# Feed-forward inputs with one 512-column matmul and one of 256 in place of three of 256, in a two-block network on one core

## The chip, the core and the metric

The kernel runs on one core of a Trainium2 chip. TensorE multiplies matrices, VectorE (DVE in the profile) and ScalarE (ACT) work on elements, GpSimd (POOL) and SyncE (SP) mostly issue transfers. The metric is the device time of one execution in microseconds, lower being better; "time" is the median of three executions.

## The reference

Two blocks of depth 2 run one after the other on an activation of 256 tokens x 1024 features in float32. Each block layer has a mixer (the first block: a bidirectional mLSTM and a dilated attention; the second: a bidirectional state-space scan and a windowed attention with grouped keys) and a gated feed-forward part. What the change touches most is the feed-forward part; in both blocks it takes two products of the same activation and multiplies them:

```python
def swiglu(u, w1, w3, w2):                       # first block
    return (jax.nn.silu(u @ w1) * (u @ w3)) @ w2

        h = rms_norm(x, norm2_w[i])              # second block
        g, u = jnp.split(h @ w_up[i], [D_FF_2], axis=-1)
        g = depthwise_conv_centered(g, ffn_conv_w[i], ffn_conv_b[i])
        x = x + (jax.nn.silu(g) * u) @ w_down[i]
```

The width of the feed-forward part is 2816, or 22 tiles of 128. The windowed attention of the second block is the other place:

```python
        s = jnp.einsum("bqgrd,bkgd->bgrqk", qb, kb,
                       preferred_element_type=jnp.float32) * scale + bias
```

with 16 query heads of 64 dimensions on 4 key heads.

## The kernel before

**Precision.** A matmul operand is split in two: `hi`, the value rounded to the type that TensorE takes in one pass (written by ScalarE), and `lo`, the rest (written by VectorE, line 473). A product is three matmuls: hi x hi, hi x lo, lo x hi (`mm3`, lines 519 to 522). The names in the profile say which is which: for weights `hi` and `lo`, for the activation of a stage `uh` and `ul`.

**Weights.** All weights come as a list of chunks of 1 MB (`raw`, three buffers), in the order of a plan (`make_plan`). `chunk` makes sure that the two chunks after the one being used have been loaded and split. Chunks of kind "ada" are reduced on VectorE (line 412) instead of being multiplied on TensorE; in the first layer there are 12 of them among the 22 + 11 chunks of the feed-forward part.

**Order.** A scheduler orders each engine's instructions when the program is built, by priority (the order in the text, moved by the tables `PRIO1` and `PRIO2`) and by when its model expects operands to be there. At run time each engine works through its list in that order. In the mixers, small steps (scores, transposes, state-space products) are put between the large linear products by hand (`tick`, `pump`).

**Feed-forward inputs.** `ffn_in` (line 1341) walks over 20 chunks (f = 2 to 21; the first two tiles come from another place). A chunk holds the two weight tiles of one f, each of 8 k-tiles of 128 x 128. `lin_st` makes both products into one PSUM bank of 512 columns (`lbank`, four of them), the first into columns 0 to 255, the second into 256 to 511, 48 matmuls of 256 columns in all, with the weight as the stationary operand and 256 tokens as the moving one. `tail` (line 1366 for the first block, 1843 for the second) then makes the gate out of the bank and writes the parts of the result (`ffh`, `ffl`). The tail's tiles have 1 KB per partition and come from buffers shared by size: five of 1 KB in the first block, four in the second (`SHARED1`, `SHARED2`).

**Feed-forward outputs.** `unit` (lines 612 to 614, bank `ffo`) makes them with the activation as the stationary operand and 512 weight columns as the moving one.

**Attention scores of the second block** (`score`, lines 1644 to 1661): `q2t` holds, for even and for odd heads, the rounded query in the head's own 64 rows and the rest of it in the other 64. `kst` holds the rounded keys in both halves, so that one matmul over 128 rows (line 1652) gives two of the three products. The third (line 1653) multiplies the own 64 rows with the rest of the keys (`kl`), which is there once.

**Groups.** The transposes of probabilities (`mpt`, `qtr`), the products of the state-space part (`sy`, line 1573), of the windowed attention (`qo`, line 1705) and of the dilated one (`ao`) are groups of small matmuls whose operands are made one after another, for head 0 before head 1, for tokens 0 to 127 before 128 to 255. "sy", "qo", "qrt" and "ao" write 64 output columns of the array per matmul; the profile shows this as a stationary operand of 128*64, where others have 128*128 and line 1653 has 64*128. A float32 operand that is not split gives two instructions per matmul.

Of the kernel before, what the change touches and what calls it, by code (L numbers as in the profile page):

```python
# [10 lines left out]
F32 = mybir.dt.float32  # L11
F32R = mybir.dt.float32r
AF = mybir.ActivationFunctionType
ALU = mybir.AluOpType
# [34 lines left out]
SHARED2 = {512: 3, 1024: 4, 2048: 11, 3072: 5, 4096: 2}  # L49

C_ID, C_TU, C_TL, C_MK = 0, 128, 256, 384
N_CST = 384 + 512
# [252 lines left out]
def two_blocks_kernel(ctx: ExitStack, tc: tile.TileContext, a: dict, out: bass.AP, stop=None):  # L305
# [7 lines left out]
    pools = ExitStack()  # L313
    cur = {"tp": pools.enter_context(tc.tile_pool(name="tmp1", bufs=2)), "shared": SHARED1}
# [33 lines left out]
    mk = cst[:, C_MK:C_MK + 512]  # L348
# [13 lines left out]
    for l in range(DEPTH):  # L362
        pv1.append(cp.tile([P, a["pv1"].shape[2]], F32, name=f"pv1_{l}"))
        pv2.append(cp.tile([P, a["pv2"].shape[2]], F32, name=f"pv2_{l}"))
        rw2.append(cp.tile([P, 80], F32, name=f"rw2_{l}"))
    S.dma_start(pv1[0], a["pv1"][0])

    def late_params():
        S.dma_start(cst[:, P:], a["cst"][:, P:])
# [153 lines left out]

    def half_views(half, n):
# [251 lines left out]
    def new_u():  # L776
        uh = big("uh", F32R)
        ul = big("ul", F32R)
        return uh, ul
# [169 lines left out]
    def mixer1(l, u, ob0=None, small=None, begun=None):  # L949
# [78 lines left out]
        def head(h, qT, kT, v):  # L1028
# [42 lines left out]
            def trans():  # L1071
                tr = bank("mpt")
                for tt in range(2):
# [129 lines left out]
        def slots(j, qk):  # L1203
# [50 lines left out]
            def pv_():  # L1254
                o = bank("ao")
                for k, g, t0, n, vk in ((0, 0, 0, T, 0), (1, 0, 0, T, 1), (0, 1, 0, P, 0), (0, 1, P, P, 1),
                                        (1, 2, 0, P, 0), (1, 2, P, P, 1)):
                    for i in range(2):
                        c0 = (2 * j + i) * 64
                        PE.matmul(o[64 * i:64 * i + 64, t0:t0 + n], va[g][:, vk, c0:c0 + 64],  # L1260
                                  s["t", i, g > 0][:, k, t0:t0 + n], start=(k, g) == (0, 0), stop=(g, t0) == (2, P))
# [79 lines left out]
    def ffn_in(kind, l, u, outs, tail, mid=None):  # L1341
        prios["now"] = {}
        for f, ps in enumerate(outs):
            tail(f, ps)
        for f in range(2, NF):
            tail(f, lin_st(chunk(kind, l, f), u)[0])
# [16 lines left out]
    def ffn1(l, u, outs):  # L1363
        act = ff_tiles()

        def tail(f, ps):
            th = tmp([T], "fth")
            S.activation(th, ps[:, :T], AF.Tanh, scale=0.5)
            V.scalar_tensor_tensor(th, th, 1.0, ps[:, :T], ALU.add, ALU.mult)
            gt = tmp([T], "fgt")  # L1370
            V.tensor_tensor(gt, th, ps[:, T:], ALU.mult)
# [68 lines left out]
    def mixer2(l, u, zouts, small):  # L1440
# [95 lines left out]
        def ssd_quarter(i, xt):  # L1536
# [26 lines left out]
            def prod(pr):  # L1563
                def run():
# [5 lines left out]
                    for d, c, m0, l0, n in ((0, 0, 0, 0, T), (1, 1, P, 0, T), (0, 1, T, P, P), (1, 0, 0, 0, P)):  # L1570
                        for k in range(2):
# [48 lines left out]
        kl = tmp([2, T], "kl", F32R)  # L1620
# [3 lines left out]
        def attn(c):  # L1624
# [17 lines left out]
            def score(i):  # L1642
                def run():
                    hd = 4 * c + i
                    p = i % 2
                    own = slice(64 * p, 64 * p + 64)
# [125 lines left out]
        def keys():  # L1772
            ps = st("k2")
            for p in range(2):
# [4 lines left out]
                V.tensor_tensor(kl[own], src, kst[p][own].bitcast(F32), ALU.subtract)  # L1779
# [59 lines left out]
    def ffn2(l, u, outs):  # L1839
# [4 lines left out]
        def tail(f, ps):  # L1844
            acc = tmp([T], "fgt")
            g0 = ps[:, :T]
# [8 lines left out]
            V.tensor_tensor(gt, th, ps[:, T:], ALU.mult)  # L1855
# [62 lines left out]
```

## Time and profile before

| | |
|---|---|
| time, median of three | 1934.13 us (1933.36 to 1936.22) |
| profiled execution | 1935.3 us |
| its span, first to last instruction | 1933.5 us |
| granted TensorE clock, mean | 0.997 of full speed |
| TensorE, matmuls | 1890.2 us busy, 13022 instructions |
| VectorE | 1465.9 us busy |
| ScalarE | 1085.0 us busy |
| moved by DMA | 388 MB, 201 GB/s on average |

A row of the profile that names a line of the kernel gives the engine, the operation, the tiles that it writes and reads, and their shapes. Matmuls overlap in the array, so the durations of neighbouring rows add up to more than the time they take; the distance from start to start is what a matmul costs. The stretches of the feed-forward inputs in the span are 394 to 509, 939 to 1057, 1348 to 1461 and 1750 to 1865 us; the main parts of the second block's mixers are 1186 to 1310 and 1586 to 1712 us.

### The profile page before, as it was taken

What the parts mean: (1) busy time and instruction counts of PE and PEld (TensorE: products, weight loads), DVE (VectorE), ACT (ScalarE), POOL (GpSimd) and SP (SyncE); (2) the same over time, 40 slices, a digit from 0 to 9 for tenths busy, and PEclk for the clock granted to TensorE, in tenths of its full rate; (3) what the DMA queues carried; (4) which work ended last, traced back from release to release, by engine and by line L of the source; (5) the groups of instructions that cost most, each with busy time, mean ns of one, the idle gap of its engine ahead of it and who ended that gap; (6) DMA issues with size and microseconds to landing.
All of it is one profiled execution on the core that took longest, in us unless ns stands there. A gap on an engine that the chain in (4) does not pass through costs nothing.

```text
span 1933.5 us, 32684 instructions
## 1 busy us (share of the span) xinstructions
PE 1890.2 (98%) x13022; PEld 1710.4 (88%) x13022; DVE 1465.9 (76%) x2555; ACT 1085.0 (56%) x1881; POOL 87.5 (5%) x108
## 2 busy tenths in 40 slices
PE   6999999999999999999999999999999999999998
PEld 5889999899978899999899888778998898779996
DVE  8888877787767787868766578877876688768763
ACT  3556654454436566544544457876554577756552
POOL 0000000200010000000200001000000000000000
PEclk9999999999999999999999999999999999999999
DMA  8654777487745446767377636444555454345552
GB/s 313 253 185 161 265 248 275 154 292 287 272 153 196 175 169 222 249 255 261 137 272 281 230 111 181 132 128 174 196 192 183 171 184 152 107 169 188 192 179 86
DMA packets 64202, 388.09 MB, mean 201 GB/s; under 512 B 7611, under 2 KB 12395, under 8 KB 21554
## 3 DMA queue, kind: packets, MB, share of 16 engines
q1 hardware_dynamic: 58064, 364.93, 52.3%
q0 software_dynamic: 4832, 20.13, 3.5%
q8 instruction: 102, 1.67, 0.3%
q10 hardware_dynamic: 1154, 0.95, 0.2%
q14 instruction: 50, 0.41, 0.1%
HBM read 384.82 MB, written 5.36 MB: 202 GB/s over the span
## 4 chain that ended last, share of the span: by engine, by line
PE 88%; DVE 5%; ACT 3%; DMA 1%; issue 1%; POOL 0%; POOLq 0%; DVEq 0%; ACTq 0%
PE lst L520 17%; PE lst L521 17%; PE lst L522 17%; PE ffo L613 4%; PE ffo L612 4%; PE ffo L614 4%; PE wo L612 2%; PE wo L613 2%; PE wo L614 2%; PE sy L1573 2%; PE qs L1653 1%; PE qo L1705 1%; PE avl L553 1%; PE avl L554 1%; PE avl L555 1%
## 5 line engine op out<-in xcount | busy, mean ns | idle before, releaser
L473 ACT ACTIVATE hi<-raw 128x1024 fp32r<-128x1024 f32 x546 | 571.7, 1057 | 499.0 <-PE lst L521 302.0
L473 DVE TENSOR_TENSOR lo<-raw,hi 128x1024 fp32r<-128x1024 f32 x546 | 662.5, 1221 | 229.5 <-ACT hi L473 228.7
L520 PE MATMUL lst<-uh,hi 128*128 128x256 f32 x2592 | 743.9, 287 | 0.0
L522 PE MATMUL lst<-uh,lo 128*128 128x256 f32 x2592 | 737.8, 285 | 0.2
L521 PE MATMUL lst<-ul,hi 128*128 128x256 f32 x2592 | 737.9, 285 | 0.0
L520 PEld LDWEIGHTS lst<-uh,hi 128*128 128x128 f32 x2592 | 496.6, 192 | 5.1 <-issue 3.9
L522 PEld LDWEIGHTS lst<-uh,lo 128*128 128x128 f32 x2592 | 496.7, 192 | 4.5 <-issue 3.5
L521 PEld LDWEIGHTS lst<-ul,hi 128*128 128x128 f32 x2592 | 496.8, 192 | 3.3 <-issue 2.1
L412 DVE CUSTOM_DVE_ANT_0 raw<-raw,crow,pv 128x1024 f32<-128x1024 f32 x96 | 120.9, 1280 | 27.6 <-DMA raw<-in_ws_dram 27.5
L612 PE MATMUL ffo<-hi,ffh 128*128 128x512 f32 x352 | 137.3, 390 | 0.0
L613 PE MATMUL ffo<-lo,ffh 128*128 128x512 f32 x352 | 137.0, 389 | 0.0
L614 PE MATMUL ffo<-hi,ffl 128*128 128x512 f32 x352 | 137.0, 389 | 0.0
L942 DVE SCALAR_TENSOR_TENSOR cacc<-cin,pv,cacc 128x254 f32<-128x254 f32 (+2 forms) x272 | 111.6, 478 | 0.3 <-ACT cacc L935 0.2
L614 PEld LDWEIGHTS ffo<-hi,ffl 128*128 128x128 f32 x352 | 66.1, 188 | 13.7
L612 PEld LDWEIGHTS ffo<-hi,ffh 128*128 128x128 f32 x352 | 66.1, 188 | 13.5
L613 PEld LDWEIGHTS ffo<-lo,ffh 128*128 128x128 f32 x352 | 66.1, 188 | 13.5
L774 DVE TENSOR_TENSOR ul<-uf,uh 128x256 fp32r<-128x256 f32 (+1 forms) x35 | 26.4, 755 | 26.7 <-ACT uh L769 26.7
L1555 ACT ACTIVATE sM<-arow,ac 128x128 f32<-128x128 f32 x128 | 44.9, 389 | 0.0
L1402 ACT ACTIVATE rsq<-xres 128x512 f32<-128x512 f32 x20 | 12.5, 627 | 53.3 <-DVE xres L1865 21.6
L553 PE MATMUL mvh<-hi,uh 128*128 128x512 f32 x80 | 33.4, 418 | 8.1 <-ACT uh L865 8.1
L555 PE MATMUL ltt<-hib,ul 128*128 128x512 f32 x72 | 29.7, 413 | 7.7 <-DVE ul L774 5.5
L766 ACT ACTIVATE uf<-tr,ub,us 128x128 f32<-128x128 f32 x36 | 14.3, 451 | 39.9 <-PE tr L752 39.9
(381 smaller groups left out, 3004.4 us busy)
## 6 DMA issues: line engine op xcount, KB each, us to landing
raw<-in_ws_dram SPq DMA_DIRECT2D x329, 1024.0 KB, 4.9
abias<-in_bt_dram SPq DMA_DIRECT2D x32, 256.0 KB, 4.7
arow<-scra POOLq DMA_DIRECT2D x32, 256.0 KB, 5.4
wtab<-skew SPq DMA_DIRECT2D x16, 384.0 KB, 3.6
gb<-in_rows_dram POOLq DMA_DIRECT2D x8, 512.0 KB, 5.8
skew<-scrt POOLq DMA_DIRECT2D x4, 1024.0 KB, 11.9
raw<-in_ws_dram SPq DMA_DIRECT2D x6, 512.0 KB, 8.9
grow<-scrg POOLq DMA_DIRECT2D x2, 1024.0 KB, 6.3
```

Of the source, the lines that this page charges most:

```text
L412: V.tensor_tensor_reduce(src, src, crow, 1.0, pv1[l][:, 136 + sec * 8 + ct:137 + sec * 8 + ct], ALU.mult, ALU.add, ada[l, sec][:, ct:ct + 1])
L473: fn()
L520: PE.matmul(outp, sh, mh, start=first, stop=False)
L521: PE.matmul(outp, sh, ml, start=False, stop=False)
L522: PE.matmul(outp, sl, mh, start=False, stop=last)
L553: PE.matmul(outs[tt], sl[0], hi[:, i, :], start=kt == first, stop=False)
L555: PE.matmul(outs[tt], sl[1], hi[:, i, :], start=False, stop=kt == last)
L612: PE.matmul(o, sh, hi[:, i, :], start=kt == first, stop=False)
L613: PE.matmul(o, sh, lo[:, i, :], start=False, stop=False)
L614: PE.matmul(o, sl, hi[:, i, :], start=False, stop=kt == last)
L942: V.scalar_tensor_tensor(acc[:, c, lo:hi], src[:, lo + s:hi + s], cw[:, k0 + j:k0 + j + 1], acc[:, c, lo:hi], ALU.mult, ALU.add)
L1555: S.activation(m[:, d, 2 * tt * P:(2 * tt + 1) * P], rt[:, d, hh, tt * P:(tt + 1) * P], AF.Relu, scale=-1.0, bias=ac[:, tt, col])
```

## The change

Three things change.

1. The activation of a stage is kept with the two parts of a k-tile side by side (`Acts`): 256 columns of the rounded part, then 256 of the rest. In `ffn_in` a new routine (`lin_wide`) multiplies the rounded weight with both at once, one matmul of 512 columns into a whole bank, and the rest of the weight with the rounded part, one of 256 columns into the first half of the bank. Each of the chunk's two products has its own bank, one from each of the two PSUM pools (four banks each). `wide_sum` then adds the two halves of a bank into a new 1 KB tile: ScalarE copies the second half, VectorE adds the first.
2. The rest of the keys (`klt`) is kept in both halves of the rows, once for even and once for odd heads, and line 1653's matmul takes all 128 rows. The tile that this needs comes from a twelfth 2 KB buffer; its space is won by putting the mask `mk` and the first block's parameters `pv1` into a pool that is given back before the second block. The mask has a transfer of its own.
3. Five groups of small matmuls run in the other order, so that their first instruction reads what is made last.

```diff
-SHARED2 = {512: 3, 1024: 4, 2048: 11, 3072: 5, 4096: 2}
+SHARED2 = {512: 3, 1024: 4, 2048: 12, 3072: 5, 4096: 2}
...
+    class Acts:
+        def __init__(self, name, n=8):
+            self.tiles = [big(name, F32R, (P, 4, 2, T)) for _ in range(n // 4)]
...
+        def both(self, kt):
+            return self.tiles[kt // 4][:, kt % 4]
...
+    def lin_wide(w, u):
+        banks = []
+        for half, pool in zip(w, (lbank, bank)):
+            hi, lo = half_views(half, P)
+            banks.append(pool("lsw"))
+            for kt in range(8):
+                with prio("lin"):
+                    PE.matmul(banks[-1], hi[:, kt, :], u.both(kt), start=kt == 0, stop=False)
+                    PE.matmul(banks[-1][:, :T], lo[:, kt, :], u[0][:, kt, :], start=False, stop=kt == 7)
+        return banks
+
+    def wide_sum(banks):
+        res = []
+        for b in banks:
+            res.append(tmp([T], "lss"))
+            S.activation(res[-1], b[:, T:], AF.Copy)
+            V.tensor_tensor(res[-1], b[:, :T], res[-1], ALU.add)
+        return res
...
-        uh = big("uh", F32R)
-        ul = big("ul", F32R)
-        return uh, ul
+        return Acts("u")
...
         for f in range(2, NF):
-            tail(f, lin_st(chunk(kind, l, f), u)[0])
+            tail(f, wide_sum(lin_wide(chunk(kind, l, f), u)))
...
-                for tt in range(2):
+                for tt in (1, 0):
                     for c in range(2):
                         PE.transpose(tr[:, c * T + tt * P:c * T + (tt + 1) * P], s["p"][:, tt, c * P:(c + 1) * P],
...
-                for k, g, t0, n, vk in ((0, 0, 0, T, 0), (1, 0, 0, T, 1), (0, 1, 0, P, 0), (0, 1, P, P, 1),
-                                        (1, 2, 0, P, 0), (1, 2, P, P, 1)):
-                    for i in range(2):
+                for k, g, t0, n, vk in ((0, 1, 0, P, 0), (0, 1, P, P, 1), (1, 2, 0, P, 0), (1, 2, P, P, 1),
+                                        (0, 0, 0, T, 0), (1, 0, 0, T, 1)):
+                    for i in (1, 0):
...
-                        for k in range(2):
+                        for k in (1, 0):
                             h = 2 * pr + k
                             PE.matmul(o[64 * k:64 * k + 64, l0:l0 + n], xd[:, d, c, 64 * h:64 * h + 64],
...
-                        PE.matmul(sp[:, tt * T:(tt + 1) * T], q[own], kl[own, kt, :], start=False, stop=True)
+                        PE.matmul(sp[:, tt * T:(tt + 1) * T], q, klt[p][:, kt, :], start=False, stop=True)
...
-                for tt in range(2):
+                for tt in (1, 0):
                     for k in range(2):
                         PE.transpose(tr[:, k * T + tt * P:k * T + (tt + 1) * P], s[i][:, tt, k * P:(k + 1) * P],
...
-                        for i in range(2):
+                        for i in (1, 0):
                             kv = 2 * (c // 2) + i
...
-                V.tensor_tensor(kl[own], src, kst[p][own].bitcast(F32), ALU.subtract)
+                for h in (own, other):
+                    V.tensor_tensor(klt[p][h], src, kst[p][own].bitcast(F32), ALU.subtract)
```

## Rows read from the trace of the kernel before

**Rows 1.** The page, busy us (share of the span) and instructions
```profile
PE 1890.2 (98%) x13022; PEld 1710.4 (88%) x13022; DVE 1465.9 (76%) x2555; ACT 1085.0 (56%) x1881; POOL 87.5 (5%) x108
```

**Rows 2.** Table by stretches: feed-forward inputs (four), second block's mixers (two)
```profile
core 0: us, PE busy (x) PEld busy (x) DVE busy (x) ACT busy (x) POOL busy (x), PEclk, DMA share, GB/s
394.00:509.00 115.00, 115.00 (x961) 114.96 (x960) 99.48 (x157) 56.53 (x85) 0.54 (x1) 1.00 0.82 296
939.00:1057.00 118.00, 117.89 (x973) 116.58 (x972) 85.95 (x125) 58.77 (x88) 4.10 (x8) 1.00 0.72 261
1348.00:1461.00 113.00, 113.00 (x944) 113.00 (x943) 90.71 (x145) 64.48 (x102) 0.00 (x0) 1.00 0.56 201
1750.00:1865.00 115.00, 114.90 (x959) 114.69 (x958) 92.70 (x147) 66.66 (x105) 0.00 (x0) 1.00 0.56 198
1186.00:1310.00 124.00, 123.97 (x841) 97.18 (x842) 101.52 (x211) 96.03 (x232) 6.72 (x12) 1.00 0.46 145
1586.00:1712.00 126.00, 124.55 (x831) 96.76 (x830) 98.58 (x199) 92.26 (x221) 6.97 (x10) 1.00 0.44 144
```

**Rows 3.** Waits of TensorE, 1186 to 1310: us in total, times, longest
```profile
PE sy L1573 <- DVE xd L1528: 1.1, 1, 1.1
```

**Rows 4.** Timeline, TensorE: start us, us; input products, first and last of 943
```profile
1348.03 0.28 PE L522 MATMUL lst<-uh,lo 128*128 128x256 f32 x1
...
1461.07 0.28 PE L522 MATMUL lst<-uh,lo 128*128 128x256 f32 x1
```

**Rows 5.** Timeline, TensorE: output products of 512 columns, first and last of 252
```profile
508.70 0.40 PE L612 MATMUL ffo<-hi,ffh 128*128 128x512 f32 x1
...
565.62 0.40 PE L614 MATMUL ffo<-hi,ffl 128*128 128x512 f32 x1
```

**Rows 6.** Timeline, TensorE: first of 24 with 512 columns, and what follows them
```profile
629.79 0.39 PE L553 MATMUL avl<-hi,uh 128*128 128x512 f32 x1
...
635.38 1.89 PE L1036 MATMUL ms<-m_k,m_q 128*128 128x256 f32 x8
```

**Rows 7.** Timeline, VectorE: start us, us; an operation from PSUM and the next
```profile
395.72 0.41 DVE L1369 SCALAR_TENSOR_TENSOR fth<-fth,lst 128x256 f32<-128x256 f32 x1
396.05 1.22 DVE L473 TENSOR_TENSOR lo<-raw,hi 128x1024 fp32r<-128x1024 f32 x1
```

**Rows 8.** Timeline, ScalarE and VectorE: one tail of the second block
```profile
1358.86 0.55 ACT L1847 ACTIVATE fgt<-lst,pv 128x256 f32<-128x256 f32 x1
...
1362.70 0.42 DVE L1853 SCALAR_TENSOR_TENSOR fth<-fth,fgt 128x256 f32<-128x256 f32 x1
...
1365.59 0.42 DVE L1858 TENSOR_TENSOR ffl<-fgu,ffh 128x256 fp32r<-128x256 f32 x1
```

**Rows 9.** Timeline, TensorE: a run of four scores and what follows
```profile
1234.32 0.39 PE L1652 MATMUL qs<-kst,q2t 128*128 128x256 f32 x1
1234.63 0.38 PE L1653 MATMUL qs<-kl,q2t 64*128 64x256 f32 x1
...
1235.57 0.39 PE L520 MATMUL lst<-uh,hi 128*128 128x256 f32 x1
1235.79 0.28 PE L521 MATMUL lst<-ul,hi 128*128 128x256 f32 x1
```

**Rows 10.** Groups by line and shape: count | busy us, mean ns | idle before
```profile
L1653 PE MATMUL qs<-kl,q2t 64*128 64x256 f32 x64 | 24.4, 380 | 0.0
```

**Rows 11.** Chain of waits, 1180 to 1186: start us, us, what
```profile
1184.56 0.69 DVE kl L1779
```

**Rows 12.** Timeline, TensorE: a lone pair of "sy" between input products
```profile
1577.14 0.28 PE L521 MATMUL lst<-ul,hi 128*128 128x256 f32 x1
1577.38 0.65 PE L1573 MATMUL sy<-sM,xd 128*64 128x256 f32 x2
...
1578.18 0.28 PE L520 MATMUL lst<-uh,hi 128*128 128x256 f32 x1
```

**Rows 13.** Waits of VectorE, 1186 to 1310: us in total, times, longest
```profile
DVE qPT L1675 <- PE qtr L1669: 4.7, 5, 2.0
```

More of the change, by code (lines that the diff above doesn't have):

```diff
@@ L347, in two_blocks_kernel @@
     triL = cst[:, C_TL:C_TL + P]
-    mk = cst[:, C_MK:C_MK + 512]
+    mk = cp1.tile([P, 512], F32, name="mk")
     ones = cp.tile([P, P], F32, name="ones")
@@ L362, in two_blocks_kernel @@
     for l in range(DEPTH):
-        pv1.append(cp.tile([P, a["pv1"].shape[2]], F32, name=f"pv1_{l}"))
+        pv1.append(cp1.tile([P, a["pv1"].shape[2]], F32, name=f"pv1_{l}"))
         pv2.append(cp.tile([P, a["pv2"].shape[2]], F32, name=f"pv2_{l}"))
@@ L368, in late_params @@
     def late_params():
-        S.dma_start(cst[:, P:], a["cst"][:, P:])
+        S.dma_start(cst[:, P:], a["cst"][:, P:N_CST])
+        S.dma_start(mk, a["cst"][:, C_MK:C_MK + 512])
         S.dma_start(pv1[1], a["pv1"][1])
@@ L522, in mm3, with __getitem__, __iter__, __init__ @@
         PE.matmul(outp, sl, mh, start=False, stop=last)
+    class Acts:
+        def __init__(self, name, n=8):
+            self.tiles = [big(name, F32R, (P, 4, 2, T)) for _ in range(n // 4)]
+        def __getitem__(self, part):
+            return Part(self.tiles, part)
+        def __iter__(self):
+            return iter((self[0], self[1]))
+        def both(self, kt):
+            return self.tiles[kt // 4][:, kt % 4]
+    class Part:
+        def __init__(self, tiles, part):
+            self.tiles, self.part = tiles, part
+        def __getitem__(self, at):
+            p, c, t = at
+            if isinstance(c, slice):
+                i = c.start // 4
+                assert (c.stop - 1) // 4 == i
+                return self.tiles[i][p, c.start - 4 * i:c.stop - 4 * i, self.part, t]
+            return self.tiles[c // 4][p, c % 4, self.part, t]
     def half_views(half, n):
@@ L1255, in pv_ @@
                 o = bank("ao")
-                for k, g, t0, n, vk in ((0, 0, 0, T, 0), (1, 0, 0, T, 1), (0, 1, 0, P, 0), (0, 1, P, P, 1),
-                                        (1, 2, 0, P, 0), (1, 2, P, P, 1)):
-                    for i in range(2):
+                for k, g, t0, n, vk in ((0, 1, 0, P, 0), (0, 1, P, P, 1), (1, 2, 0, P, 0), (1, 2, P, P, 1),
+                                        (0, 0, 0, T, 0), (1, 0, 0, T, 1)):
+                    for i in (1, 0):
                         c0 = (2 * j + i) * 64
                         PE.matmul(o[64 * i:64 * i + 64, t0:t0 + n], va[g][:, vk, c0:c0 + 64],
-                                  s["t", i, g > 0][:, k, t0:t0 + n], start=(k, g) == (0, 0), stop=(g, t0) == (2, P))
+                                  s["t", i, g > 0][:, k, t0:t0 + n], start=(g, t0) == (1, 0), stop=(k, g) == (1, 0))
                 for tt in range(2):
@@ L1343, in ffn_in @@
         for f, ps in enumerate(outs):
-            tail(f, ps)
+            tail(f, (ps[:, :T], ps[:, T:]))
         for f in range(2, NF):
-            tail(f, lin_st(chunk(kind, l, f), u)[0])
+            tail(f, wide_sum(lin_wide(chunk(kind, l, f), u)))
             if mid and f == 10:
@@ L1367, in tail @@
             th = tmp([T], "fth")
-            S.activation(th, ps[:, :T], AF.Tanh, scale=0.5)
-            V.scalar_tensor_tensor(th, th, 1.0, ps[:, :T], ALU.add, ALU.mult)
+            S.activation(th, ps[0], AF.Tanh, scale=0.5)
+            V.scalar_tensor_tensor(th, th, 1.0, ps[0], ALU.add, ALU.mult)
             gt = tmp([T], "fgt")
-            V.tensor_tensor(gt, th, ps[:, T:], ALU.mult)
+            V.tensor_tensor(gt, th, ps[1], ALU.mult)
             fh, fl = act(f)
@@ L1619, in mixer2 @@
         kst = [tmp([2, T], f"kst{p}", F32R) for p in range(2)]
-        kl = tmp([2, T], "kl", F32R)
+        klt = [tmp([2, T], f"klt{p}", F32R) for p in range(2)]
         vv = tmp([2, 256], "m_k")
@@ L1645, in run @@
                     p = i % 2
-                    own = slice(64 * p, 64 * p + 64)
                     kt = c // 2
@@ L1845, in tail @@
             acc = tmp([T], "fgt")
-            g0 = ps[:, :T]
+            g0 = ps[0]
             S.activation(acc, g0, AF.Identity, scale=cw[:, 3 * f + 1:3 * f + 2], bias=cb_[:, f:f + 1])
@@ L1854, in tail @@
             gt = tmp([T], "fgu")
-            V.tensor_tensor(gt, th, ps[:, T:], ALU.mult)
+            V.tensor_tensor(gt, th, ps[1], ALU.mult)
             fh, fl = act(f)
```

3 lines of the change are left out of this document (2 added, 1 removed).

## The prediction, made before the changed kernel was run

> **What bounds the kernel now.** I read the page's busy times first: TensorE's row is busy for 98% of the span [rows 1]. A busy row alone does not make a bound, so the second view is the table by stretches [rows 2]: in the four stretches that make the feed-forward inputs, and in the main parts of the second block's two mixers, TensorE is busy for all of the time, less a microsecond or so, while VectorE holds 73% to 87%. The third view asks who waits: in the first of those mixer stretches TensorE waited 1.1 us in all for anybody [rows 3]. So in all six stretches the order of matmuls is the clock, and an edit is worth what it takes off the distance from the start of one matmul to the start of the next. The duration column does not say that: matmul rows overlap. I read starts.
>
> **Part 1, wide feed-forward inputs.** Per k-tile and half of a weight chunk, three matmuls of 256 columns become one of 512 and one of 256. That is 4 layers x 20 chunks x 16 = 1280 times. Price of 256 columns: 943 matmuls of this very kind start from 1348.03 to 1461.07 without a break [rows 4], 113.04/942 = 0.1200 us. Price of 512: the output products, whose moving operand is also a plain run of 512, give 252 starts from 508.70 to 565.62 [rows 5], 56.92/251 = 0.2268 us. So three cost 0.3600, and the pair costs 0.3468: **13.2 ns each, 16.9 us in all**, 4.2 per layer. The cheapest reading: two narrow ones cost 0.2400 and a wide one 0.2268, so some 13 ns stick to each matmul instruction, whatever its columns. The other bound is the dearest wide run of the trace, 24 starts from 629.79 to the next matmul at 635.38 [rows 6], 5.59/24 = 0.2329 us; then the pair saves 7.1 ns, 9.1 us in all. Those take a stationary operand with a step of two, which the new ones do not, so I take 0.2268.
>
> The Trainium skill, page "TensorE: Matmul & The Clock Gate", section "Back-to-back issue gap", speaks against this: it gives a warm start-to-start distance of N/2.4 + 2.5 ns, so an estimate from it is 2.6 ns saved per pair and 3 us in all instead of 17. The trace disagrees by its 0.1200 and 0.2268, and the sum goes by the trace.
>
> What the halves cost: per chunk two copies on ScalarE and two additions on VectorE. A VectorE operation with this shape and a PSUM source holds the queue 0.33 us (395.72 to 396.05) [rows 7], so 40 x 0.33 = 13.3 us per layer. Three of the layers have room: the stretches have 118, 113 and 115 us, less 4.2, against 86.0, 90.7 and 92.7 + 13.3 on VectorE [rows 2], 88% to 96% full. The first layer, which also works off adaptive-norm weights on VectorE, has 99.5 + 13.3 = 112.8 against 115 - 4.2 = 110.8: **full**. Its overflow of 2 us can hide, because four PSUM banks per half let the tails fall behind by chunks before TensorE must stop, and the output products that follow ask for the last tile only near the end of their first half. I take 2 off: **-15 us**. ScalarE, busy 57 to 67 of some 115 us, has room for 40 x 0.4 more.
>
> A second cover is narrower. The tail's tiles are 1 KB; the new sums take two more of them per chunk, so the second block needs five per chunk from four buffers. The next chunk's first copy then waits until the gate product (line 1853) has freed a buffer. In the trace, from the tail's first instruction (1358.86) to the end of that product (1362.70 + 0.42) are 4.26 us [rows 8]; a copy and an addition in front make some 5.1, under the 5.55 of a new chunk (16 x 0.3468). It fits, by half a microsecond: I cost it at nothing, and it is a rival below.
>
> **Part 2, keys with all 128 rows.** The scores' second matmul used 64 rows; now it has 128, by a second copy of the keys' remainder. In the trace a run of four costs, from its start at 1234.32 to the second matmul behind it at 1235.79, 1.47 us [rows 9], where five starts at 0.120 would be 0.60: **0.87 us per four**. The first matmul after the 64-row one is late too (0.22). There are 64 of the 64-row matmuls [rows 10] and as many before them, 32 fours. Counted along the timeline, about half of them border on matmuls with 64 output columns, where one change of shape stays, whose price is an entry and an exit of some 0.1 each; I give them 0.65. 16 x 0.87 + 16 x 0.65 = **24.3 us of TensorE time**. The remainder's subtraction is doubled on VectorE, 0.69 us on the chain at 1184.56 [rows 11], with the products of the first state-space quarter behind it: **+1 us**, between 0, if it hides there, and 3, if all four added ones lie on the chain.
>
> **Part 3, the reversed loops.** They let a group's first matmul wait for the operand that is made last. Then the group is issued in one piece, where now a pair starts as soon as its operand is there, and other work is put between. Price of such a piece, from the last matmul before it (1577.14) to the second start behind it (1578.18) [rows 12]: 1.04 us, less 2 x 0.120 for the ordinary matmuls and 2 x 0.120 for its own work: 0.56 us. Both mixers together have 51 excursions to the 64-column shape, and 15 are such a lone pair of "sy" or "qo". If each joins its group 8.4 us go, if none nothing; neighbours of other kinds will still break in, so I take 11: **6.2 us of TensorE time**. In the first block the same groups already stand in one piece (all 8 of "ao"); the reversal is worth nothing there. A later first start could cost a wait, but TensorE waits for nothing to speak of [rows 3].
>
> **What of parts 2 and 3 arrives.** 30.5 us of TensorE time is 15 per mixer: 124 becomes 109. VectorE has 101.5 of work in that stretch [rows 2], and ScalarE 96. VectorE's largest wait there is for TensorE (4.7) [rows 13] and shrinks with it, so it just fits, but at 93% full with queues in order some new waits must come. I take four fifths: **-24 us**. Below, half (15); above, all of it with all 15 pieces joined (33).
>
> **Neutral parts.** The mask and the first block's parameters move to a pool that is closed before the second block; that pays for the twelfth 2 KB buffer, which the second remainder tile takes, so the rotating buffers stay as many. The mask has its own transfer on ScalarE's queue, whose issue lies behind the chunk splits at the start: nothing, at most one issue slot.
>
> **Sum.** -15 + 1 - 24 = -38 us. The profiled execution took 1935.3 us (span 1933.5 and 1.8 around it), 1.2 above the median of the runs; it becomes 1897, the median **1896 us**.
>
> **Rivals.**
> (a) VectorE becomes the mixers' bound and the feed-forward of layer 1: parts 2 and 3 bring half or less, 10 to 15 us, and part 1 some 12. For it: 93% and 101% full. Against: VectorE's largest wait is for TensorE [rows 13], and its idle time is there to be used. 1907 to 1912. Chance 0.17.
> (b) The fixed cost does not belong to the instruction: with the dearer wide run of rows 6 part 1 is worth 9 less 2, with columns alone nothing. 1904 to 1911. For it: rows 6. Against: rows 5 has ten times as many starts and the same kind of operand. Chance 0.10. By the rule of the Trainium skill's page "TensorE: Matmul & The Clock Gate", section "Back-to-back issue gap", the total would be an estimate of 1910, which lies in this case.
> (c) Slower: the four 1 KB buffers serialise the second block's tails. If a chunk's tail had to end before the next begins, its length would be the period: 1358.86 to 1365.59 + 0.42 is 7.15 [rows 8], with copy and addition 8.0 us against 5.76 now. Over 20 chunks that is 45 us per layer, less two chunks (11 us) that the banks absorb: 34, twice; with the gains elsewhere (7 of part 1, 23 of the mixers) 1934 + 68 - 30 = 1972. It decides from a period of 6.1 on (below it the banks absorb it all), and turns the whole change slower from about 7.1. Against it: the buffers come free in order, before the tail's end. Chance 0.04.
> (d) More than thought, every piece joins and nothing new waits: 1880 to 1886. Chance 0.06.
> The forecast, 1886 to 1905, has the rest, 0.63.
>
> **Numbers.** The range reaches from 1884 (16.9 and 33 with nothing lost) to 1912 (7 and 15). Faster 0.94, within 0.2% (4 us, about what a measurement of this kernel tells from no change) 0.02, slower 0.04.
>
> **What would show it.** Right: the wide matmuls start 0.227 us apart from the narrow ones behind them, an input chunk takes 5.55 us where it took 5.76, the fours of scores take 0.48, no 64-row matmul is left, "sy" and "qo" stand in runs of 16 and 8, and the mixer stretches shrink by 12 us each with VectorE over 90% busy. Wrong: a wide matmul at 0.233 or 0.240, gaps on TensorE's row in the input stretches that wait for the weights' remainder or for a bank, or mixers in which TensorE waits for VectorE by more than 4 us.

## The result: 22 us faster, where 38 were forecast, and the profile after

The changed kernel takes **1911.31 us** (median, 1910.6 to 1915.09) against 1933.74 us (1932.4 to 1936.22) of the kernel before on the same chip: a ratio of 0.9886, 95% interval 0.9869 to 0.9904. The forecast was 1896. The profiled execution has a span of 1909.9 us, against 1933.5.

The page of the changed kernel, first the busy times (compare [rows 1]), then two of the new groups of instructions (busy us, mean ns of one | idle time before them and what ended it):

```profile
PE 1851.2 (97%) x11742; PEld 1630.1 (85%) x11742; DVE 1521.2 (80%) x2719; ACT 1132.8 (59%) x2041; POOL 88.1 (5%) x108
...
L583 PE MATMUL lsw<-u,hi 128*128 128x512 f32 x1280 | 450.7, 396 | 10.0 <-DVE lss L592 10.0
...
L591 ACT ACTIVATE lss<-lsw 128x256 f32<-128x256 f32 x160 | 58.5, 374 | 54.2 <-DVE fth L1901 33.4
```

1280 matmuls are gone and VectorE has 55 us more to do, as the change says. What is new is on the right: TensorE stands idle for 10.0 us ahead of a wide input matmul until VectorE has added two halves (L592), and ScalarE's copy of a half (L591) stands idle for 33.4 us until VectorE has made the gate product of the second block (L1901). The table by stretches of the changed kernel says where (the five stretches are the first five of [rows 2], shifted and cut to the shorter stages; columns as there):

```profile
394.00:501.00 107.00, 107.00 (x617) 93.65 (x616) 105.01 (x179) 66.76 (x120) 0.00 (x0) 1.00 0.82 301
939.00:1047.00 108.00, 108.00 (x609) 92.79 (x608) 90.52 (x152) 65.12 (x118) 2.48 (x5) 1.00 0.74 269
1330.00:1449.00 119.00, 113.45 (x644) 97.72 (x642) 99.28 (x166) 74.46 (x131) 0.00 (x0) 1.00 0.53 195
1723.00:1841.00 118.00, 112.72 (x639) 97.28 (x639) 98.10 (x165) 73.48 (x129) 0.00 (x0) 1.00 0.55 197
1184.00:1292.00 108.00, 105.64 (x819) 88.58 (x819) 98.76 (x205) 92.76 (x228) 6.96 (x11) 1.00 0.54 171
```

In the first block's feed-forward inputs TensorE has no gap, even in layer 1 where VectorE is busy for 105.0 of 107 us. In the second block's it lacks 5 us in each layer: 119 and 118 us for what was to be 111. I cut both spans at the same landmarks (the norm that closes each stage, read from the chain of waits) and added up the stages:

| stage | before, us | after, us | difference | forecast |
|---|---|---|---|---|
| first block, both mixers | 724.9 | 725.6 | +0.7 | 0 |
| first block, feed-forward, layers 1 and 2 | 194.8, 204.6 | 191.6, 202.9 | -3.1, -1.7 | -2.2, -4.2 |
| second block, mixers, layers 1 and 2 | 205.3, 214.9 | 193.7, 199.2 | -11.5, -15.7 | -23 in all |
| second block, feed-forward, layers 1 and 2 | 189.1, 200.1 | 192.9, 204.0 | **+3.8, +3.9** | -4.2, -4.2 |

(The forecast of part 1 is laid out here per layer, with its 2 us of overflow in the first.) The mixers gave more than forecast. The second block's feed-forward was to lose 8 us and gained 8: that is 16 us, more than the miss of 15 to the median. The mixers' 4 us beyond the forecast hide a part of it.

The waits of TensorE in that stretch of layer 1, 1330 to 1452 us (us in total, times, longest):

```profile
PE lsw L583 <- DVE lss L592: 5.0, 7, 0.8
PE ffo L662 <- DVE lss L592: 0.8, 1, 0.8
```

And the loop behind it, one period of the changed kernel's timeline (start us, us; in brackets the idle time before and what ended it), VectorE, then ScalarE, then the starts of three chunks on TensorE:

```profile
1426.85 1.23 DVE L475 TENSOR_TENSOR lo<-raw,hi 128x1024 fp32r<-128x1024 f32 x1 [0.89 <-ACT hi L475]
1428.00 0.42 DVE L1901 SCALAR_TENSOR_TENSOR fth<-fth,fgt 128x256 f32<-128x256 f32 x1
...
1428.86 0.42 DVE L592 TENSOR_TENSOR lss<-lsw,lss 128x256 f32<-128x256 f32 x1
...
1433.47 1.23 DVE L475 TENSOR_TENSOR lo<-raw,hi 128x1024 fp32r<-128x1024 f32 x1 [0.85 <-ACT hi L475]
1434.61 0.42 DVE L1901 SCALAR_TENSOR_TENSOR fth<-fth,fgt 128x256 f32<-128x256 f32 x1
...
1428.45 0.38 ACT L591 ACTIVATE lss<-lsw 128x256 f32<-128x256 f32 x1 [1.32 <-DVE fth L1901]
1428.73 1.05 ACT L475 ACTIVATE hi<-raw 128x1024 fp32r<-128x1024 f32 x1
1429.68 0.41 ACT L1905 ACTIVATE ffh<-fgu 128x256 fp32r<-128x256 f32 x1
1429.98 0.38 ACT L591 ACTIVATE lss<-lsw 128x256 f32<-128x256 f32 x1
1430.25 0.60 ACT L1895 ACTIVATE fgt<-lss,pv 128x256 f32<-128x256 f32 x1
1432.37 1.06 ACT L475 ACTIVATE hi<-raw 128x1024 fp32r<-128x1024 f32 x1 [1.52 <-PE lsw L583]
1433.34 0.40 ACT L1900 ACTIVATE fth<-fgt 128x256 f32<-128x256 f32 x1
1435.07 0.38 ACT L591 ACTIVATE lss<-lsw 128x256 f32<-128x256 f32 x1 [1.32 <-DVE fth L1901]
...
1429.43 0.47 PE L583 MATMUL lsw<-u,hi 128*128 128x512 f32 x1 [0.77 <-DVE lss L592]
1436.05 0.47 PE L583 MATMUL lsw<-u,hi 128*128 128x512 f32 x1 [0.82 <-DVE lss L592]
1442.70 0.47 PE L583 MATMUL lsw<-u,hi 128*128 128x512 f32 x1 [0.77 <-DVE lss L592]
```

Read it as a ring. The copy at 1428.45 starts when the gate product L1901 of the tail before it has ended (1428.00 + 0.42) and so given a 1 KB buffer back. Its sum leads to the gate (1430.25), the tanh (1433.34) and the next L1901 (1434.61), and that one lets the next copy go at 1435.07: 6.62 us. In the ring stand, in queue order: on ScalarE a weight split (1428.73), the rounding of the tail before (1429.68) and the chunk's second copy (1429.98) ahead of the gate, and another split (1432.37) ahead of the tanh; on VectorE a split (1433.47) ahead of the gate product. TensorE starts chunks at 1429.43, 1436.05 and 1442.70, 6.62 and 6.65 us apart, instead of 5.55. It does so only for the last seven of the twenty chunks (from 1402.92 on): the tails are slow from the start (a chunk's second copies go from 1351.31 to 1449.86 in 15 periods of 6.57 on average; the early ones vary between 5.7 and 7.0, and the shortest is still above 5.55), and the four banks per half take up the lag of the first dozen.

### The profile page after: what moved, and what is told of

Its sections match the earlier page's. It is cut to its first block, busy times and chain, and to the rows that moved or that the text cites. A ratio compares the mean times of both kernels' runs of the same rounds, so it can differ in the third digit from the quotient of the medians.

```text
span 1909.9 us, 30411 instructions
## 1 busy us (share of the span) xinstructions
PE 1851.2 (97%) x11742; PEld 1630.1 (85%) x11742; DVE 1521.2 (80%) x2719; ACT 1132.8 (59%) x2041; POOL 88.1 (5%) x108
## 4 chain that ended last, share of the span: by engine, by line
PE 83%; DVE 7%; ACT 5%; DMA 3%; issue 2%; POOL 0%; POOLq 0%; DVEq 0%; ACTq 0%
PE lsw L583 14%; PE lst L522 8%; PE lst L523 8%; PE lst L524 8%; PE lsw L584 7%; PE ffo L662 4%; PE ffo L664 4%; PE ffo L663 4%; PE wo L662 2%; DMA raw<-in_ws_dram 2%; PE wo L663 2%; PE wo L664 2%; ACT hi L475 2%; DVE lo L475 1%; PE sy L1621 1%
## 5 line engine op out<-in xcount | busy, mean ns | idle before, releaser
L583 PE MATMUL lsw<-u,hi 128*128 128x512 f32 x1280 | 450.7, 396 | 10.0 <-DVE lss L592 10.0
L522 PE MATMUL lst<-u,hi 128*128 128x256 f32 x1312 | 380.3, 290 | 0.0
L523 PE MATMUL lst<-u,hi 128*128 128x256 f32 x1312 | 374.4, 285 | 0.0
L524 PE MATMUL lst<-u,lo 128*128 128x256 f32 x1312 | 374.3, 285 | 0.0
L584 PE MATMUL lsw<-u,lo 128*128 128x256 f32 x1280 | 359.2, 281 | 0.2
L583 PEld LDWEIGHTS lsw<-u,hi 128*128 128x128 f32 x1280 | 239.9, 187 | 70.0 <-PE lsw L584 14.1
L522 PEld LDWEIGHTS lst<-u,hi 128*128 128x128 f32 x1312 | 251.1, 191 | 3.3 <-issue 2.4
L523 PEld LDWEIGHTS lst<-u,hi 128*128 128x128 f32 x1312 | 251.2, 191 | 2.0 <-issue 1.2
L524 PEld LDWEIGHTS lst<-u,lo 128*128 128x128 f32 x1312 | 251.1, 191 | 1.3 <-issue 1.1
L584 PEld LDWEIGHTS lsw<-u,lo 128*128 128x128 f32 x1280 | 241.8, 189 | 0.8 <-DVE lo L475 0.8
L414 DVE CUSTOM_DVE_ANT_0 raw<-raw,crow,pv 128x1024 f32<-128x1024 f32 x96 | 121.2, 1280 | 21.2 <-DMA raw<-in_ws_dram 21.0
L591 ACT ACTIVATE lss<-lsw 128x256 f32<-128x256 f32 x160 | 58.5, 374 | 54.2 <-DVE fth L1901 33.4
L592 DVE TENSOR_TENSOR lss<-lsw,lss 128x256 f32<-128x256 f32 x160 | 65.4, 420 | 1.4 <-ACT lss L591 1.1
```

The costliest lines, as they stand in the source:

```text
L414: V.tensor_tensor_reduce(src, src, crow, 1.0, pv1[l][:, 136 + sec * 8 + ct:137 + sec * 8 + ct], ALU.mult, ALU.add, ada[l, sec][:, ct:ct + 1])
L522: PE.matmul(outp, sh, mh, start=first, stop=False)
L523: PE.matmul(outp, sh, ml, start=False, stop=False)
L524: PE.matmul(outp, sl, mh, start=False, stop=last)
L583: PE.matmul(banks[-1], hi[:, kt, :], u.both(kt), start=kt == 0, stop=False)
L584: PE.matmul(banks[-1][:, :T], lo[:, kt, :], u[0][:, kt, :], start=False, stop=kt == 7)
```

## The experiments

Each kernel ran beside the kernel before on its chip; the ratio is against that, with a 95% interval. The medians of the kernel before were 1933.7 to 1934.3 us.

### One more 1 KB buffer

The changed kernel, with one number changed:

```diff
-SHARED2 = {512: 3, 1024: 4, 2048: 12, 3072: 5, 4096: 2}
+SHARED2 = {512: 3, 1024: 5, 2048: 12, 3072: 5, 4096: 2}
```

> The changed kernel with five instead of four 1 KB buffers in the second block, nothing else. Theory A (the four buffers bind the second block's tails: ScalarE's copy into the first sum waits until line 1901's product of the chunk before has freed one, 1.3 us each): the chunk period of the second block's feed-forward inputs falls from 6.65 to 5.55-5.65 us, TensorE no longer waits for the sums, each such layer is 7 to 8 us shorter, 1911 becomes 1895 to 1898. Theory B (VectorE is simply full there with 13 us more work): the period stays above 6.4 and the time at 1908 to 1912.

Measured: **1896.84 us** (1893.89 to 1898.59), ratio 0.9805 (0.979 to 0.982). The table by stretches for the second block's first feed-forward inputs in this kernel, and then ScalarE's waits there:

```profile
1329.00:1440.00 111.00, 111.00 (x642) 97.77 (x642) 100.70 (x176) 79.55 (x138) 0.00 (x0) 1.00 0.57 206
```

```profile
ACT lss L591 <- DVE fth L1901: 13.2, 17, 1.1
```

TensorE is busy for all of 111 us, every chunk behind the first takes 5.55, and no wait of TensorE is left there. VectorE does the same work in 8 us less and is 91% busy, so it was not the bound: the buffer was. The copy still waits for the gate product, but now a period of 5.55 goes through it. The two stages fell to 184.8 and 195.8 us, 8 less each than after the change, and 4.3 less than before it: part 1's gain as the prediction had it.

### Six buffers

```diff
-SHARED2 = {512: 3, 1024: 4, 2048: 12, 3072: 5, 4096: 2}
+SHARED2 = {512: 3, 1024: 6, 2048: 12, 3072: 5, 4096: 2}
```

> The changed kernel with six 1 KB buffers in the second block. Theory A (five tiles per chunk need five buffers, and with five the tails already keep up): the same as with five, 1894 to 1898, chunk period 5.55 us. Theory C (the tails still lag with five, only hidden by the PSUM banks): some microseconds less than with five, at the starts of the output products.

Measured: 1896.52 us (1892.58 to 1897.39), ratio 0.9801 (0.9787 to 0.9816). No more than with five, though the copy's wait for L1901 is gone here. ScalarE now waits one step on, 15.4 us in all, for the product behind it (L1903): idle time of an engine that is not the bound, worth nothing.

### Part 1 alone

The kernel before with `Acts`, `lin_wide` and `wide_sum`, but the old scores and the old order of the groups.

```diff
-            tail(f, lin_st(chunk(kind, l, f), u)[0])
+            tail(f, wide_sum(lin_wide(chunk(kind, l, f), u)))
```

> The kernel before with part 1 alone (wide matmuls and halves; the attention and the order of groups as before, four 1 KB buffers). If the stage lengths of the changed kernel belong to part 1, the feed-forward parts of the first block give 3 + 2 us and those of the second lose 4 + 4: 1934 becomes 1934 to 1939, no gain. If instead the losses of the second block's feed-forward come from the other parts (a schedule pushed out of place), part 1 alone gives its forecast 15 us: 1919.

Measured: 1937.33 us (1935.22 to 1939.89), ratio 1.002 (1.001 to 1.003): by itself, part 1 makes the kernel slower by 4 us. TensorE's waits in the second block's inputs are the same 5.0 us in 7 times, and the chunks go from 5.55 to 6.65 us in the same way. The two first-block stages fall by 2.2 and 3.3 us, the two second-block ones grow by some 4 each. The ring is part 1's own, then, and neither of the other parts shares in it.

### Part 2 alone

The kernel before with the rest of the keys on all 128 rows (and the twelfth 2 KB buffer).

```diff
-                        PE.matmul(sp[:, tt * T:(tt + 1) * T], q[own], kl[own, kt, :], start=False, stop=True)
+                        PE.matmul(sp[:, tt * T:(tt + 1) * T], q, klt[p][:, kt, :], start=False, stop=True)
```

> The kernel before with part 2 alone (keys' remainder in all 128 rows, the pools that it needs). By the sum of the prediction 24 us of TensorE time in the two mixers, four fifths of it arriving: 1934 - 19 = 1915, mixers 9 to 10 us shorter each. By the rival (VectorE binds the mixers) half: 1922.

Measured: **1910.89 us** (1909.46 to 1911.73), ratio 0.9878 (0.9864 to 0.9893). The second block's mixers fall by 11.6 and 13.2 us, 24.8 in all, and no other stage moves by more than 2.1. In the kernel before, 3.4 us at the end of the second mixer ran at the lower clock (granted clock 0.50 from 1711.6 to 1715.0), and none did here; by an estimate from these two numbers that is 1.7 of the 24.8. The median fell by 22.9. The prediction had 24.3 us of TensorE's time for it: nearly all of it arrives, not four fifths. A run of four scores in the changed kernel (TensorE's timeline), beside [rows 9]:

```profile
1202.37 0.36 PE L1699 MATMUL qs<-kst,q2t 128*128 128x256 f32 x1
1202.57 0.28 PE L1700 MATMUL qs<-klt,q2t 128*128 128x256 f32 x1
1202.69 0.28 PE L1699 MATMUL qs<-kst,q2t 128*128 128x256 f32 x1
1202.81 0.28 PE L1700 MATMUL qs<-klt,q2t 128*128 128x256 f32 x1
```

The starts are 0.12 us apart (0.20 behind the first, which follows a transpose), the distance of ordinary matmuls of 256 columns [rows 4], where the 64-row ones stood 0.31 apart. The Trainium skill, page "TensorEngine Tiling (Array Packing)", section "Key Properties", says that a change of tiling mode drains the engine; the pairs of rows agree in direction, 0.31 with a change between neighbours and 0.12 without.

### Part 3 alone

```diff
-                        for k in range(2):
+                        for k in (1, 0):
                             h = 2 * pr + k
```

and the other four reversals of the change.

> The kernel before with part 3 alone (reversed loops). By the sum 6 us of TensorE time (11 lone pairs of 15 join, 0.56 us each): 1928 to 1930; nothing in the first block. If the reversal costs waits of TensorE instead, 1934 to 1938.

Measured: 1929.01 us (1927.47 to 1932.92), ratio 0.9975 (0.9966 to 0.9985): 4.8 us faster, near the 6.2 that were worked out. The second block's mixers move by +1.5 and -7.7. Their excursions to the 64-column shape (runs of matmuls with a stationary operand of 128*64), counted on the timeline, fall from 25 + 34 to 19 + 24, and the lone pairs of "sy" or "qo" among them from 16 to 4: 12 joined, where 11 were assumed. The lower clock plays into both mixers: the 3.4 us of it in the second mixer of the kernel before are gone, and 3.4 us stand towards the end of the first mixer here (from 1307.9).

### The change without part 3, five buffers

The kernel of the first experiment, with all five reversals undone.

```diff
-                        for k in (1, 0):
+                        for k in range(2):
                             h = 2 * pr + k
```

> The changed kernel with five 1 KB buffers and without part 3 (loops in the order of before). If part 3's gain adds to the other parts (4.8 us alone): 1900 to 1903. If part 2 has taken away most of what part 3 saves, or its new waits of TensorE eat the rest: 1895 to 1899.

Measured: 1896.6 us (1895.76 to 1897.31), ratio 0.9806 (0.9791 to 0.982): the same as with part 3. Yet part 3 does what it says here too: 17 + 25 excursions with it, 24 + 36 without, by the same count. Where did that go? The whole first mixer of the second block, with part 3 (first row) and without it (second), in the table by stretches:

```profile
1116.00:1312.00 196.00, 187.50 (x1367) 162.81 (x1367) 168.24 (x339) 143.90 (x320) 14.04 (x22) 0.99 0.47 157
```

```profile
1117.00:1312.00 195.00, 190.58 (x1375) 165.15 (x1374) 169.43 (x342) 144.63 (x320) 13.51 (x22) 1.00 0.48 159
```

TensorE works 3.1 us less with part 3 and is idle for 8.5 us instead of 4.4. Its waits with part 3 include two that are not there without it:

```profile
PE wo L662 <- ACT mixah L1760: 1.5, 1, 1.5
PE grs L1657 <- POOL grt L383: 0.8, 1, 0.8
```

With fewer pieces to fit in, the planner issues the mixer's output products ("wo") earlier: 1.5 us are lost at 1276.7 when they have run ahead of their operand, and at the mixer's end none are left to lie over the group norm (0.8, and two more waits of 0.4). Behind the first of these gaps the granted clock goes down. The table by stretches of the kernel with part 3:

```profile
1275.00:1280.00 5.00, 3.50 (x22) 2.60 (x22) 4.39 (x8) 5.00 (x9) 0.01 (x1) 1.00 0.59 213
1280.00:1284.00 4.00, 4.00 (x22) 2.44 (x20) 3.23 (x4) 0.95 (x2) 1.61 (x1) 0.57 0.44 141
1284.00:1289.00 5.00, 5.00 (x33) 3.90 (x30) 2.74 (x4) 1.58 (x2) 0.00 (x0) 1.00 0.81 308
```

From 1280 to 1284 us it is 0.57 of full speed on average, so most of the time at the lower level, 1.2 GHz; three output products there start 0.43 us apart instead of 0.23. Without part 3 the same part of the mixer has neither these gaps nor the low clock. So what the joined pieces save in this mixer is given back. The waits belong to the reversed loops: all four stand in every kernel here that has parts 2 and 3 in this layer, and none of them in the kernels whose loops in this layer run in the old order. That the earlier output products are what opens them is read from the rows; the last experiments bear on it.

The changed kernel, with its four buffers, tells the gaps and the clock apart. It has the same gap, 1.49 us ahead of an output product at 1281.30, and the same waits at the mixer's end. But the granted clock stays at 1.00, and the mixer takes 193.7 us, against 193.8 for the kernel without part 3. Its table by stretches, around the gap and behind it:

```profile
1280.00:1284.00 4.00, 2.70 (x24) 2.21 (x26) 3.40 (x5) 4.00 (x6) 0.87 (x1) 1.00 0.64 250
1284.00:1300.00 16.00, 14.42 (x80) 10.87 (x77) 12.96 (x23) 7.88 (x11) 1.45 (x2) 1.00 0.39 134
```

So the gaps alone use up the saving, and with five buffers the stretch at the lower clock comes on top: 196.1 us. The gap by itself does not bring the lower clock; what does is open. In the second layer's mixer part 3 gains 2.4 us here (199.3 against 201.7), although a second such stretch (granted clock 0.51 from 1676.3 to 1679.7) falls into it with part 3 and none without.

### Wide matmuls first, narrow ones behind them

Five buffers, and within a half of a chunk eight wide matmuls, then eight narrow ones.

```diff
                     PE.matmul(banks[-1], hi[:, kt, :], u.both(kt), start=kt == 0, stop=False)
+            for kt in range(8):
+                with prio("lin"):
                     PE.matmul(banks[-1][:, :T], lo[:, kt, :], u[0][:, kt, :], start=False, stop=kt == 7)
```

> The changed kernel with five 1 KB buffers; in a half chunk all eight 512-column matmuls stand first, then all eight of 256 columns. Tells whether a chunk's two periods (5.55 and 5.65 us, flipping where TensorE does something else in between) come from the alternation of the two widths. If they do: one period everywhere, 16 x (0.2268 + 0.1200) = 5.55 us by the prediction's prices, and 1 to 2 us less than with the alternation. If not: both periods are seen again, time 1895 to 1899.

What it is about: alternating pairs have two periods. In the changed kernel, layer 1 of the first block, TensorE's timeline ahead of an interruption by other matmuls and behind it:

```profile
431.77 0.39 PE L583 MATMUL lsw<-u,hi 128*128 128x512 f32 x1
432.00 0.28 PE L584 MATMUL lsw<-u,lo 128*128 128x256 f32 x1
432.12 0.39 PE L583 MATMUL lsw<-u,hi 128*128 128x512 f32 x1
...
443.56 1.04 PE L426 MATMUL adag<-cst,adap 128*128 128x128 f32 x8
...
445.13 0.40 PE L583 MATMUL lsw<-u,hi 128*128 128x512 f32 x1
445.36 0.28 PE L584 MATMUL lsw<-u,lo 128*128 128x256 f32 x1
445.48 0.40 PE L583 MATMUL lsw<-u,hi 128*128 128x512 f32 x1
445.72 0.28 PE L584 MATMUL lsw<-u,lo 128*128 128x256 f32 x1
445.84 0.40 PE L583 MATMUL lsw<-u,hi 128*128 128x512 f32 x1
```

Over longer runs a pair takes 0.3466 us ahead of the eight transposes and 0.3533 behind them (431.77 to 432.12, and 445.13 to 445.84 for two), and it stays so to the end of this stage. Over a chunk of 16 pairs that is 5.55 against 5.65 us.

Measured: 1893.89 us (1893.54 to 1895.96), ratio 0.9795 (0.9779 to 0.9812). One half chunk of its timeline, and the start of the next:

```profile
1361.96 2.00 PE L583 MATMUL lsw<-u,hi 128*128 128x512 f32 x8
1363.80 1.11 PE L586 MATMUL lsw<-u,lo 128*128 128x256 f32 x8
1364.75 2.00 PE L583 MATMUL lsw<-u,hi 128*128 128x512 f32 x8
```

Eight wide ones take 1.84 us (0.230 each), eight narrow ones 0.95 (0.119), a half chunk 2.79; and 2.79 it is in all four layers, behind interruptions too. That is 5.59 per chunk, not the 5.55 expected: a little more than the faster period and less than the slower. The median is 3 us under the first experiment's, but the intervals of the two ratios overlap, and in the profiled executions the four feed-forward stages add up to 774.3 us here and 773.8 there. So a gain by the grouping is not shown.

### Interruptions on purpose

Five buffers, with one, two, three and four transposes of the identity put behind chunks 6, 10, 14 and 18 of the second block's inputs. Their result goes nowhere.

```diff
+            if kind == "up" and f in (6, 10, 14, 18):
+                dum = bank("dum")
+                for c in range((f - 2) // 4):
+                    PE.transpose(dum[:, c * P:(c + 1) * P], ident, ident)
```

> The changed kernel with five 1 KB buffers; in the second block's feed-forward inputs one, two, three and four transposes of the identity (results unused) are put behind chunks 6, 10, 14 and 18. Tells what turns the chunk period from 5.55 to 5.65 us: without them all chunks of these two layers took 5.55. If any interruption of the stream can turn it, some of the stretches between the transposes run at 5.65 and others at 5.55. If it is tied to the first block (its tiles' places, the transfers there), all stay at 5.55.

Measured: 1898.36 us (one execution). In both layers the chunks take 5.55 us up to the single transpose, 5.58 and 5.64 with it and right behind it, and 5.55 again two chunks later; from the two transposes on they take 5.65 to 5.66 and never come back, apart from the interrupted chunks and the ones right behind them. In the first experiment, without interruptions, all behind the first are 5.55. So an interruption of TensorE's stream is enough to change the period for good, and which interruption does it is not a matter of the kind of instruction alone; whether it is the number of transposes or their place, one run with both changing together can't say. The change goes the other way too: with part 1 alone, the first block's second layer runs at 5.65 us ahead of its interruption and at 5.55 behind it. Why there are two periods stays open.

### Grouped, with part 3 only in the last mixer's loops, or not at all

Both are the grouped kernel with five buffers. In the first, the second block's loops are reversed only in its second layer, where part 3 alone had brought 7.7 us (one of the three loops is shown):

```diff
-                        for k in (1, 0):
+                        for k in (1, 0) if l else (0, 1):
                             h = 2 * pr + k
```

> Five 1 KB buffers, a half chunk's eight wide matmuls ahead of its eight narrow ones, and in the second block the reversed loops in its second layer alone. Theory D (the reversed loops save TensorE time in both mixers, but in the first layer's the output products are used up early as filler and the group norm at its end stands uncovered, some 4 us with a fallen clock; in the second layer more is saved than lost): 1 to 3 us under the version with both layers reversed, 1891 to 1893, and the first mixer without the waits at its end. Rival (the difference between the versions is scatter of the schedule): 1893 to 1896.

Measured: **1892.21 us** (1891.65 to 1894.12), ratio 0.979 (0.9775 to 0.9804), the lowest of all. In the second, no loop is reversed (one of the five is shown):

```diff
-                        for k in (1, 0):
+                        for k in range(2):
                             h = 2 * pr + k
```

> The same without any reversed loop. Theory D: the first mixer as in the version with the second layer alone reversed, the second mixer 2 to 3 us longer, 1893 to 1896. Rival: no difference between the two.

Measured: 1895.01 us (1894.61 to 1895.99), ratio 0.9803 (0.9787 to 0.982). The second block's mixers, in us:

| grouped, five buffers | layer 1 | layer 2 |
|---|---|---|
| all reversed | 196.2 | 197.7 |
| reversed in layer 2 alone | 194.8 | 197.7 |
| none reversed | 193.9 | 201.8 |

Reversing is worth 4 us in layer 2 and costs 1 to 2 in layer 1. In the last two kernels the gap of 1.5 us and the waits at the first mixer's end are gone, and with them the stretch at the lower clock (from 1291.5 with all reversed). Both differences have the sign that the gaps of the sixth experiment give; but layer 1, which has the old order in both last kernels, still differs by 0.9 us between them. So only the 4 us of layer 2 can be called shown.

## Why the prediction was off, step by step

**Inside the range, by luck.** 1911.31 lies 0.7 us under the upper end of the range, 1912, and in the 1907 to 1912 of rival (a). Both stood for causes that did not come: a dearer wide matmul, half of the mixers' gain, VectorE as the bound. What made the time is one term that the sum had at nothing.

**The price of a pair: right.** Wide and narrow took 0.3466 us together; 0.3468 was the sum, from output products that the inputs were to resemble. So the saving of some 13 ns for the matmul that is gone arrived, as long as the stream keeps its faster period. By the rule of the Trainium skill, page "TensorE: Matmul & The Clock Gate", section "Back-to-back issue gap", N/2.4 + 2.5 ns, which the section gives for an isolated matmul, the pair would be an estimate of 325 ns and the old three 328; the measured 346.6 against 360 decides, as in the prediction.

**VectorE full in layer 1: right in size, and cheaper than thought.** 105.0 of 107 us busy against the 112.8 of 110.8 that was worked out, with no gap on TensorE. The 2 us of overflow were not lost. What the first block's layers lack of their 4.2 us is about the second period, 0.1 us per chunk, which no row of before could show: they gave 3.1 and 3.0 with five buffers, where the chunks behind an interruption in mid-stage have it, and 3.1 and 1.7 in the changed kernel, where in layer 2 all chunks have it.

**The failed step: the cover that was costed at nothing.** "It fits, by half a microsecond: I cost it at nothing." The four 1 KB buffers did not fit. The prediction took the 4.26 us of a tail in [rows 8], added one copy and one addition, and set 5.1 against 5.55. The ring takes 6.6. Its error is not in a duration but in what was put in the ring. The copy and the addition were to take 0.84 us; from the copy to the gate it is 1.80 (1428.45 to 1430.25), because a split, a rounding and the second copy stand in between on ScalarE. With the 4.26 that alone makes 6.1. From the gate to the end of L1901 it is 4.78 instead of 4.26 (1430.25 to 1434.61 + 0.42): the split ahead of the tanh waits 1.52 us for TensorE to give a weight buffer back, and by then TensorE itself waits for the sums. A latency read while the queues had room was used as one in a ring where they have none. Half a microsecond of slack on a ring through the queues of several engines was no cover, and it was the one step on which 8 us per layer hung.

**The rival for it was named, and mis-sized.** Case (c) has the right mechanism, place and point: four buffers, the second block, "decides from a period of 6.1 on". The period was 6.6, not its 8.0, so a layer took 3.8 us more than before, not 34 (the same arithmetic gives 6 at a period of 6.6), and the change did not turn slower. Its chance of 0.04 stood for the extreme alone; there was no case between "free" and 8.0, and the range reached to 1912 for other reasons. With the fifth buffer the forecast holds, 1896.84 against 1896, and so does part 1's share of it: 14.7 us in the four stages.

**Parts 2 and 3: the sum nearly right, its two halves wrong against each other.** Forecast -23, measured -27.2 with the change and -24.8 with five buffers. Part 2's 24.3 us of TensorE time arrives nearly whole (24.8 between two executions, some 23 without the kernel before's stretch at the lower clock), so the factor of four fifths was wrong for it; VectorE, 98.8 of 108 us busy, was not the bound, and rival (a) fell. Part 3's 6.2 is near right by itself (4.8), and in sum nothing on top of part 2 (1896.84 against 1896.6): with all loops grouped by width, 4 us gained in layer 2 stand against 1 to 2 lost in layer 1. By the count used above the kernel before has 59 excursions and 16 lone pairs, where the prediction counted 51 and 15; its 11 that join were 12. The cause of a loss was looked for in VectorE; it came from the order, on TensorE, where the prediction had written that a later start could cost a wait and dismissed it on [rows 3]. That view shows the waits that the old order leaves; it says nothing of what a new order uncovers. The microsecond for the doubled subtraction of the keys is not to be seen in these sums.

**Rivals (b) and (d)** are out: the pair's price leaves no room for (b), and even the best version stays above 1886.

**Open:** the +1.0 us of the first block's first mixer, where the change moves the mask's transfer and the order of two groups, and no experiment took it apart; among the kernels here that stage takes 370.6 to 373.8 us, so it is within that scatter. Open too is what brings the stretches of 3.4 us at the lower clock. Between the first 40 us and the last 12 of the span, the kernel before has one of them, the changed kernel two, and the kernel with part 2 alone none.

## What to carry to other kernels

An edit that puts one more tile per step through a shared pool closes a ring from the tile's last reader to the next step's first writer: write down everything that stands in each queue on that way, other work's instructions too, or give the pool one buffer more; here half a microsecond of margin was none, and that one number was worth 14.5 us. Time that a bound engine saves can arrive nearly in full (part 2) even with its neighbour 91% busy, but pieces that serve as filler are also cover for something: before they are joined, look for the wait they lie over. And test parts both alone and on top of each other: part 1 was worth nothing without the buffer, and part 3, once part 2 was there, was worth something only in the second layer.

## What the chip showed that was not expected

Alternating matmuls of 512 and 256 columns run in one of two steady periods, 0.3466 or 0.3533 us per pair, and an interruption by a few short matmuls can move the stream from the first to the second, where it stays for the rest of the stage, or from the second to the first; grouped by width they keep to 2.79 us per eight pairs, which is 0.349 each. And with five buffers a gap of 1.5 us on TensorE was followed, some 2 us after it, by 3.4 us at the lower clock, while in the changed kernel a gap of the same length in the same place was followed by none, so the gap alone does not account for the clock.
